# Dealing channel blocks to SBUF partitions so that a transfer's parts walk through neighbouring blocks of HBM

## The chip, the cores and the metric

One core of one Trainium2 chip. The time is the device time of one execution in microseconds; medians are given with the number of runs. Runs carry a state: a run over 1.5% above the fastest of its kernel is called slow, the others fast; a single run on one core has the state "unknown". Each run has its own runs of the kernel before on the same chip beside it; those medians lay between 91.2 and 91.4 us.

## The reference

An im2col with a 3 x 3 window: for each image and channel, nine shifted copies of the 30 x 30 window positions.

```python
batch, c, h, w = (16, 64, 32, 32)          # float32, kernel_size = 3
for i in range(h_out):                      # 30
    for j in range(w_out):                  # 30
        cols[b, :, i * w_out + j] = x[b, :, i:i + 3, j:j + 3].ravel()
# cols: (16, 64 * 9, 900)
```

No arithmetic: 4.19 MB come in, 33.18 MB go out.

## The kernel before

The 1024 channel planes (16 images x 64 channels) are cut into 128 blocks of eight planes. Partition p holds block p. A block is 32,768 B in x and 259,200 B in the output. Two loads bring two planes and then six planes of every block into SBUF. Then, four times, VectorE and ScalarE copy the nine shifted views of two planes per partition into an output tile, and one transfer sends the tile out: one contiguous run of 64,800 B for each partition. Output tiles have two buffers. SyncE issues all six transfers.

```python
x_v = x.rearrange("b (cp c2) h w -> (b cp) (c2 h w)", c2=CPP)                  # CPP = 8
out_v = out.rearrange("b (cp c2 kk) n -> (b cp) c2 (kk n)", c2=CPP, kk=KK)

def load(r0, r1):
    return nc.sync.dma_start(out=in_flat[:, r0 * W : r1 * W],
                             in_=x_v[:, r0 * W : r1 * W])
first = load(0, 2 * H)
load(2 * H, CPP * H)

for c in range(0, CPP, 2):
    out_tile = out_pool.tile([P, 2, KK, HO, WO], x.dtype, name="out_tile")
    # ... cut: ScalarE and VectorE copy the shifted views of planes c and c + 1 ...
    nc.sync.dma_start(
        out=out_v[:, c : c + 2].rearrange("p c n -> p (c n)"),
        in_=out_tile.rearrange("p c kk i j -> p (c kk i j)"),
    )
# ... cut: the first load is moved ahead of the program's start-up barrier ...
```

In the built program every transfer has two plain dimensions on both sides, 128 rows of one run each. For an output (step and count, in elements, slowest first):

```
HBM  [[64800, 128], [1, 16200]]      SBUF  [[16200, 128], [1, 16200]]
```

Of the kernel before, what the change touches and what calls it, by code (L numbers as in the profile page):

```python
# [1 line left out]

# [3 lines left out]


def _im2col(ctx, tc, x, K, out):


    nc = tc.nc
    P = nc.NUM_PARTITIONS

    B, C, H, W = x.shape
    HO = H - K + 1
    WO = W - K + 1
    KK = K * K
    assert out.shape == (B, C * KK, HO * WO)
    CPP = B * C // P
    assert CPP * P == B * C and C % CPP == 0 and CPP % 2 == 0 and K == 3  # L20

    x_v = x.rearrange("b (cp c2) h w -> (b cp) (c2 h w)", c2=CPP)
    out_v = out.rearrange("b (cp c2 kk) n -> (b cp) c2 (kk n)", c2=CPP, kk=KK)

    in_pool = ctx.enter_context(tc.tile_pool(name="in_pool", bufs=1))
    out_pool = ctx.enter_context(tc.tile_pool(name="out_pool", bufs=2))

    ctx.enter_context(tc.manual_schedule())

    in_tile = in_pool.tile([P, CPP, H, W], x.dtype, name="in_tile")  # L30
    in_flat = in_tile.rearrange("p c h w -> p (c h w)")

    def load(r0, r1):

        return nc.sync.dma_start(
            out=in_flat[:, r0 * W : r1 * W],
            in_=x_v[:, r0 * W : r1 * W],
        )

    first = load(0, 2 * H)  # L40
    load(2 * H, CPP * H)

    def planes(c, ki, kj, n, step):

        w = in_tile[:, c, ki : ki + HO, kj : kj + WO]
        part, row, col = [list(d) for d in w.ap]
        return bass.AP(w.tensor, w.offset, [part, [step, n], row, col])

    for c in range(0, CPP, 2):
        out_tile = out_pool.tile([P, 2, KK, HO, WO], x.dtype, name="out_tile")  # L50


        for s in range(2):
            o = out_tile[:, s]
            nc.scalar.copy(out=o[:, K : 2 * K], in_=planes(c + s, 1, 0, K, 1))  # L55
            for ki in (0, 2):
                nc.vector.tensor_copy(  # L57
                    out=o[:, ki * K : ki * K + 2], in_=planes(c + s, ki, 0, 2, 1)
                )
            if s == 0:  # L60
                nc.vector.tensor_copy(  # L61
                    out=o[:, 2:KK:6], in_=planes(c + s, 0, 2, 2, 2 * W)
                )
            else:
                nc.vector.tensor_copy(  # L65
                    out=o[:, 2], in_=in_tile[:, c + s, 0:HO, 2 : 2 + WO]
                )
                nc.scalar.copy(  # L68
                    out=o[:, 8], in_=in_tile[:, c + s, 2 : 2 + HO, 2 : 2 + WO]
                )  # L70
        nc.sync.dma_start(  # L71
            out=out_v[:, c : c + 2].rearrange("p c n -> p (c n)"),
            in_=out_tile.rearrange("p c kk i j -> p (c kk i j)"),
        )
    return first


def kernel(
    tc: tile.TileContext,
    x: bass.AP,  # L80
    kernel_size: bass.AP,
    out: bass.AP,
):
    with ExitStack() as ctx:
        first = _im2col(ctx, tc, x, int(kernel_size), out)


    tc.close()
    tc.compile()  # L89
    blocks = tc.nc.main_func.blocks  # L90
    load = first.ins
    home = next(b for b in blocks if any(i.name == load.name for i in b.instructions))
    home.instructions = [i for i in home.instructions if i.name != load.name]
    head = list(blocks[0].instructions)
    at = next(
        k
        for k, i in enumerate(head)
        if i.engine == load.engine and type(i).__name__ == "InstDrain"
    )
    head.insert(at, load)  # L100
    blocks[0].instructions = head


# [1 line left out]
_INS = ['x', 'kernel_size']  # L105
_OUTS = [((16, 576, 900), 'float32')]

_NUMBERS = {'kernel_size': 3}


# [26 lines left out]
```

## Time and profile before

| | before |
|---|---|
| time, median of 6 runs | 91.19 us (91.10 to 91.30) |
| span of the profiled run | 89.6 us |
| DMA packets of the first load, 8,192 B, mean | 378 ns |
| DMA packets of the second load, 24,576 B, mean | 912 ns |
| DMA packets of the outputs, 64,800 B, mean | 2397 ns |

The packet durations come from the trace's records of single packets: 128 data packets per transfer, eight for each of the 16 engines. They can be checked from any DMA view of a window: (share of 16 engines) x 16 x (length of the window) / (packets). The lines below are the DMA view of the kernel before, from 5 to 11 us, where only the second load runs. The columns of the second line are packets, MB and share.

```profile
DMA packets 108, 2.65 MB, mean 442 GB/s; under 512 B 0, under 2 KB 0, under 8 KB 0
q1 hardware_dynamic: 108, 2.65, 102.6%
```

1.026 x 16 x 6 us / 108 is 0.912 us. (A share can be over 100% because a packet is counted whole where it starts.)

The time from issue to landing, from the page, and the waits of VectorE for a free output buffer (total, times, longest):

```profile
out_dram<-out_tile SPq DMA_DIRECT2D x4, 8100.0 KB, 32.4
in_tile<-in_x_dram SPq DMA_DIRECT2D x1, 3072.0 KB, 11.4
DVE out_tile L57 <- DMA out_dram<-out_tile: 27.1, 2, 13.6
```

An output transfer is under way for 19.15 us; for the rest of the 32.4 us it lay in the queue behind the one before it.

### The profile page before, as it was taken

What the parts mean: (1) busy time and instruction counts of PE and PEld (TensorE: products, weight loads), DVE (VectorE), ACT (ScalarE), POOL (GpSimd) and SP (SyncE); (2) the same over time, 40 slices, a digit from 0 to 9 for tenths busy, and PEclk for the clock granted to TensorE, in tenths of its full rate; (3) what the DMA queues carried; (4) which work ended last, traced back from release to release, by engine and by line L of the source; (5) the groups of instructions that cost most, each with busy time, mean ns of one, the idle gap of its engine ahead of it and who ended that gap; (6) DMA issues with size and microseconds to landing.
All of it is one profiled execution on the core that took longest, in us unless ns stands there. A gap on an engine that the chain in (4) does not pass through costs nothing.

```text
span 89.6 us, 96 instructions
## 1 busy us (share of the span) xinstructions
DVE 22.6 (25%) x24; ACT 23.8 (27%) x13; POOL 0.2 (0%) x4
## 2 busy tenths in 40 slices
DVE  0079759900000099500000399100000000000000
ACT  5079759900000099500000399100000000000000
POOL 0000000000000000000000000000000000000000
DMA  5989899999999999947999999999999982999990
GB/s 128 505 384 494 362 463 463 463 463 463 463 463 463 463 463 463 434 174 318 463 463 463 463 463 463 463 463 463 463 463 463 463 347 116 463 463 463 463 463 0
DMA packets 864, 37.37 MB, mean 417 GB/s; under 512 B 96, under 2 KB 96, under 8 KB 96
## 3 DMA queue, kind: packets, MB, share of 16 engines
q1 hardware_dynamic: 864, 37.37, 97.2%
HBM read 4.19 MB, written 33.18 MB: 417 GB/s over the span
## 4 chain that ended last, share of the span: by engine, by line
DMA 49%; DVE 12%; DVEq 1%; issue 0%; SPq 0%
DMA out_dram<-out_tile 36%; DMA in_tile<-in_x_dram 13%; DVE out_tile L57 8%; DVE out_tile L61 2%; DVE out_tile L65 1%; DVEq L89 1%; DVEq L57 0%; SPq L71 0%
## 5 line engine op out<-in xcount | busy, mean ns | idle before, releaser
L55 ACT COPY out_tile<-in_tile 128x2700 f32<-128x2700 f32 x8 | 19.2, 2443 | 31.7 <-DMA out_dram<-out_tile 27.1
L57 DVE COPY out_tile<-in_tile 128x1800 f32<-128x1800 f32 x16 | 16.8, 1092 | 33.7 <-DMA out_dram<-out_tile 27.1
L61 DVE COPY out_tile<-in_tile 128x1800 f32<-128x1800 f32 x4 | 4.4, 1090 | 0.0
L68 ACT COPY out_tile<-in_tile 128x900 f32<-128x900 f32 x4 | 3.8, 938 | 0.0
L65 DVE COPY out_tile<-in_tile 128x900 f32<-128x900 f32 x4 | 2.5, 620 | 0.0
L55 ACT ACT_TABLE_LOAD x1 | 1.3, 1283 | 0.8 <-PEq L118 0.8
L118 POOL MEMSET const-bfloat16-1.0<- 128x1 bf16 x1 | 0.1, 101 | 0.0
L118 POOL MEMSET const-uint8-127<- 128x1 uint8 x1 | 0.1, 101 | 0.0
L118 POOL MEMSET const-float32-0.0<- 128x1 f32 x1 | 0.1, 98 | 0.2 <-issue 0.2
L118 POOL MEMSET const-float32-1.0<- 128x1 f32 x1 | 0.1, 98 | 0.0
## 6 DMA issues: line engine op xcount, KB each, us to landing
out_dram<-out_tile SPq DMA_DIRECT2D x4, 8100.0 KB, 32.4
in_tile<-in_x_dram SPq DMA_DIRECT2D x1, 3072.0 KB, 11.4
in_tile<-in_x_dram SPq DMA_DIRECT2D x1, 1024.0 KB, 4.9
```

Of the source, the lines that this page charges most:

```text
L55: nc.scalar.copy(out=o[:, K : 2 * K], in_=planes(c + s, 1, 0, K, 1))
L57: nc.vector.tensor_copy(out=o[:, ki * K : ki * K + 2], in_=planes(c + s, ki, 0, 2, 1))
L61: nc.vector.tensor_copy(out=o[:, 2:KK:6], in_=planes(c + s, 0, 2, 2, 2 * W))
L65: nc.vector.tensor_copy(out=o[:, 2], in_=in_tile[:, c + s, 0:HO, 2 : 2 + WO])
L68: nc.scalar.copy(out=o[:, 8], in_=in_tile[:, c + s, 2 : 2 + HO, 2 : 2 + WO])
L89: tc.compile()
L118: nc = _bacc.Bacc("TRN2", target_bir_lowering=False, num_devices=1)
```

## The change

The intent: let the 16 engines work in neighbouring blocks of HBM at each moment instead of eight blocks apart. It assumes that a transfer is cut into sixteen parts of eight neighbouring rows, one part for each engine; the traces show 128 data packets per transfer and the 16 engines busy 97.2% of the span, not which rows an engine takes. Partition 8a+b now owns block 16b+a. The core of the diff:

```diff
-    x_v = x.rearrange("b (cp c2) h w -> (b cp) (c2 h w)", c2=CPP)
-    out_v = out.rearrange("b (cp c2 kk) n -> (b cp) c2 (kk n)", c2=CPP, kk=KK)
+    CP = C // CPP
+    A = 16
+    x_v = x.rearrange("(b1 b0) (cp c2) h w -> (b0 cp) b1 (c2 h w)", b0=A // CP, c2=CPP)
+    out_v = out.rearrange(
+        "(b1 b0) (cp c2 kk) n -> (b0 cp) b1 c2 (kk n)", b0=A // CP, c2=CPP, kk=KK
+    )
...
-            in_=x_v[:, r0 * W : r1 * W],
+            in_=x_v[:, :, r0 * W : r1 * W],
...
-            out=out_v[:, c : c + 2].rearrange("p c n -> p (c n)"),
+            out=out_v[:, :, c : c + 2].rearrange("a b c n -> a b (c n)"),
```

The output transfer is now:

```
HBM  [[64800, 16], [1036800, 8], [1, 16200]]      SBUF  [[16200, 128], [1, 1], [1, 16200]]
```

## The prediction

The prediction and the expectations say "ports" for an assumption: that two parts of a transfer can share something on their way and then take about twice as long. It is the second of the prediction's rivals. No trace or run names a port or tells what is shared. By "the engine's rate" they mean the 27.16 GB/s per engine that the prediction works out from the packet records; what sets this rate, no run shows.

> **What bounds the kernel now.** I read four views in this order: the page (shares of the span), the chain of waits, the waits of the issuing queue beside the timeline of the issues, and the DMA view cut to windows, down to the records of the single packets.

> The page first: the span, the busy shares, the DMA rows, the queue, the bytes.

> ```profile
> span 89.6 us, 96 instructions
> DVE 22.6 (25%) x24; ACT 23.8 (27%) x13; POOL 0.2 (0%) x4
> DMA  5989899999999999947999999999999982999990
> GB/s 128 505 384 494 362 463 463 463 463 463 463 463 463 463 463 463 434 174 318 463 463 463 463 463 463 463 463 463 463 463 463 463 347 116 463 463 463 463 463 0
> q1 hardware_dynamic: 864, 37.37, 97.2%
> HBM read 4.19 MB, written 33.18 MB: 417 GB/s over the span
> ```

> Both compute engines idle three quarters of the time; the 16 DMA engines are busy 97.2% of the span. The dips in the two DMA rows (around slices 18 and 33) are a matter of where a slice's edge falls: a packet is counted where it starts, all engines start a packet almost together, and so a slice may hold none.

> Next the chain that ended last:

> ```profile
> 0.79 11.40 DMA in_tile<-in_x_dram
> 17.95 32.59 DMA out_dram<-out_tile
> 55.77 0.54 DVE out_tile L65
> ```

> The chain names DVE for part of the way, but that is only how it walks back through semaphores. The test is whether the queue ever ran dry, and the waits of the queue with the timeline answer it:

> ```profile
> SPq L71 <- DVE out_tile L65: 54.0, 4, 18.9
> 10.69 46.03 SPq L71 DMA_DIRECT2D out_dram<-out_tile  x4
> ```

> The four output transfers are issued between 10.69 us and 56.7 us. The packet records put the end of the third transfer at 69.1 us, so the fourth lay in the queue for over 12 us before its turn; the second was issued at 17.95 us and started at 30.7. Only the first output is not covered: issued at 10.69, its first packets start at 11.54, while the last packets of the load end between 11.24 and 11.83. There is no room worth having in compute or waits.

> Last, the DMA view of a piece of the output phase:

> ```profile
> DMA packets 64, 4.15 MB, mean 415 GB/s; under 512 B 0, under 2 KB 0, under 8 KB 0
> q1 hardware_dynamic: 64, 4.15, 95.7%
> ```

> That is the window from 20 to 30 us: 64 packets took 95.7% of 16 x 10 us, or 2.39 us each. The single records agree and say more. Each transfer has 128 data packets, one per partition, eight per engine. Output packets of 64,800 B: median 2393 ns, smallest 2388, largest 2433, over all 512. Packets of the second load, 24,576 B: 912 ns, every one of the 128. Packets of the first load, 8,192 B: 309 ns for most, but 20 or so at the start take 324 to 1147 ns.

> Three sizes lie on one straight line: (2393 - 912) ns over (64,800 - 24,576) B is 27.16 GB/s per engine, and with that rate each size leaves about 7 ns fixed (912 - 905; 309 - 302; 2393 - 2386). HBM reads and HBM writes have the same rate and no scatter.[...]

> The sum per engine: mean start 1.18 us; first load 3.02 (8 x 309 = 2.47, plus 0.55 of slow first packets); second load 8 x 0.912 = 7.30; outputs 4 x 8 x 2.397 (the mean) = 76.72; semaphore packets 0.05. That gives 88.27 us, against a last packet at 88.15 to 88.33 us in the records. Another 1.3 us of landing and end make the span of 89.6, and 1.5 us outside it make the 91.12.

> [...]96 semaphore packets over 6 transfers show 16 now.[...]

> **The change part by part.** Removed: nothing; added: nothing. The same two loads and four outputs, copies, waits and buffers. What moves is which channel block lies in which partition: 8p..8p+7 style runs give way to block 16b+a in partition 8a+b. In HBM each packet is the same contiguous run (8,192, 24,576 or 64,800 B). The HBM pattern gets one dimension more, 16 x 8 x run.

> - Output packets: 32 per engine x 2393 ns either way. Best case they lose their scatter, 0.08 us in sum per engine (mean over median). Expected: 0.
> - Second load: 8 x 912 ns, no scatter to lose. Expected: 0.
> - First load: 0.55 us of slow first packets. If these are a start-up latency, they stay. If the 16 engines' first addresses collide in HBM, neighbouring blocks (32 KiB apart in x) may change it either way. I take -0.1, at most -0.55. This is on the path: everything queues behind it.
> - Issue: an issue takes 332 to 382 ns on the queue now, and 1.01 us pass from the first issue to the first packet. [...]only the first issue is on the path (the others have 0 to 12 us of cover): +0.05.
> - Copies: unchanged, 22.6 and 23.8 us, under the DMA.

> Sum: 91.12 - 0.1 + 0.05 = 91.07, say 91.0.

> **The rivals.**

> First, locality in HBM pays: the intent of the change. Against it: [...]packets have no scatter. It can be worth only the start, 0.55 + 0.08: 90.5 us, 0.7% faster, still "same".

> [...]The new HBM pattern has 16 outermost, so the hardware may cut the transfer into sixteen runs of eight partitions, 8a to 8a+7 (as the words of the change suppose)[...].[...] Packets of about 4.8 us, the DMA's 87.1 us twice: about 178 us.[...] Against it: if the present 128 partitions are already cut into such runs, then the present trace shows that it costs nothing[...]. I give this, with milder forms of it, 8%.

> Third, the neighbouring blocks collide in HBM.[...] Were the loads to run at half rate, 10.3 us more: 101 us.[...] I give it 4%.

> Fourth, fewer engines or smaller packets[...]. The run is contiguous as before and two outer dimensions remain; I give it under 1%.

> **Range and chances.** The mechanism leaves 90.5 (all start-up scatter gone) to 91.7 (a slower first load and start by 0.5 us), and the kernel's own runs scatter by 0.1. So 91.0, with a range of 90.5 to 91.7. Faster by over 2% would need 1.8 us, three times what is not already at the engines' rate: 1%. Slower by over 2%: 12%, from the second and third rivals. Within 2%: 87%.

> **What would show it.** Right: the output packets stay at 2.39 us and the second load's at 0.91, the queue's share of the span stays at 97%, four outputs of 19.15 us each follow each other without a gap, and the second output lands about 32 us after its issue. Only the first 3 us may differ. Wrong: packets longer than these. If output packets lie near 4.8 us throughout, it is the ports; if they scatter, or if only the loads are longer, it is HBM; if there are other than 16 semaphore packets per transfer, the split[...].

## The result, and the profile after

| | before | after |
|---|---|---|
| time, median of 6 runs | 91.19 us | 169.31 us (166.97 to 170.51) |
| ratio of the fast runs, 95% interval | | 1.845 (1.834 to 1.857) |
| packets of 8,192 B, mean | 378 ns | 596 ns |
| packets of 24,576 B, mean | 912 ns | 1885 ns |
| packets of 64,800 B, mean (smallest, largest) | 2397 ns (2388, 2433) | 4420 ns (2391, 5346) |

Ratios are the mean time of one kernel's fast runs over that of the other's fast runs of the same rounds, so not quite the ratio of the medians. Three of the six runs of the changed kernel are labelled slow, only because its runs scatter by 2%; the granted clock was 1.0 in all of them.

The page of the changed kernel, as far as it answers to the lines shown of before:

```profile
span 167.3 us, 96 instructions
DVE 22.6 (14%) x24; ACT 23.8 (14%) x13; POOL 0.2 (0%) x4
DMA  7998999999896999998996998898999999699910
GB/s 157 282 188 188 188 496 248 248 248 248 170 186 139 310 186 248 248 248 186 201 232 186 310 217 186 217 310 186 201 217 294 217 248 232 232 279 248 217 62 31
q1 hardware_dynamic: 864, 37.37, 96.4%
HBM read 4.19 MB, written 33.18 MB: 223 GB/s over the span
```

The compute engines did exactly the same work. The DMA engines were again busy nearly all the time (96.4%), with the same 864 packets and the same bytes, at half the rate. So no work was added and the DMA engines did not stand idle: the packets became longer. The busy share counts a packet as busy however long it takes, and so it does not show this.

Now the DMA views of three windows of the changed kernel: 8 to 18 us (second load), 40 to 50 us (first output) and 100 to 150 us.

```profile
DMA packets 93, 2.29 MB, mean 229 GB/s; under 512 B 0, under 2 KB 0, under 8 KB 0
q1 hardware_dynamic: 93, 2.29, 110.4%
...
DMA packets 31, 2.01 MB, mean 201 GB/s; under 512 B 0, under 2 KB 0, under 8 KB 0
q1 hardware_dynamic: 31, 2.01, 98.2%
...
DMA packets 200, 11.92 MB, mean 238 GB/s; under 512 B 16, under 2 KB 16, under 8 KB 16
q1 hardware_dynamic: 200, 11.92, 100.3%
```

The same sum as above gives 1.90 us per packet of the second load, 5.07 us per output packet early on, and later, with 184 data packets (16 of the 200 are semaphore packets), 4.36 us. The records show the same: 1.92 us is the commonest value in the second load, 5.05 us in the outputs. Both are 2.1 times the values of before. One engine then moves 64,800 B / 5.056 us = 12.8 GB/s, and 16 engines 205 GB/s. Later the parts come out of step: the last packet of the first output ended between 54.5 and 55.8 us over the engines, of the last output between 157.3 and 166.2 us.

The issue and the waits, to be held against the lines of before:

```profile
out_dram<-out_tile SPq DMA_DIRECT2D x4, 8100.0 KB, 66.3
in_tile<-in_x_dram SPq DMA_DIRECT2D x1, 3072.0 KB, 21.0
0.00 1.89 SPq L41 DMA_DIRECT2D in_tile<-in_x_dram  x2
DVE out_tile L63 <- DMA out_dram<-out_tile: 60.8, 2, 32.5
```

VectorE's waits more than doubled, but as an effect: it waits for buffers that the transfers release later.

Where the 77.7 us of span come from, per engine in the mean: the first packet starts at 1.54 instead of 1.18 us (+0.36); the first load takes 4.77 instead of 3.02 us (+1.75); the second 15.08 instead of 7.30 (+7.78); the outputs 141.43 instead of 76.72 (+64.71); and the last engine ends 3.36 us after the mean engine instead of 0.10 (+3.26). Together +77.9, with 0.15 us less between the last packet and the end of the span.

### The profile page after: what moved, and what is told of

Its sections match the earlier page's. It is cut to its first block, busy times and chain, and to the rows that moved or that the text cites. A ratio compares the mean times of both kernels' runs of the same rounds, so it can differ in the third digit from the quotient of the medians.

```text
span 167.3 us, 96 instructions
## 1 busy us (share of the span) xinstructions
DVE 22.6 (14%) x24; ACT 23.8 (14%) x13; POOL 0.2 (0%) x4
## 2 busy tenths in 40 slices
DMA packets 864, 37.37 MB, mean 223 GB/s; under 512 B 96, under 2 KB 96, under 8 KB 96
## 3 DMA queue, kind: packets, MB, share of 16 engines
q1 hardware_dynamic: 864, 37.37, 96.4%
HBM read 4.19 MB, written 33.18 MB: 223 GB/s over the span
## 4 chain that ended last, share of the span: by engine, by line
DMA 30%; another core or an unknown queue 19%; DVE 10%; DVEq 1%; issue 0%; SPq 0%
DMA out_dram<-out_tile 26%; DVE out_tile L63 7%; DMA in_tile<-in_x_dram 4%; DVE out_tile L67 2%; DVE out_tile L71 1%; DVEq L95 1%; DVEq L63 0%; SPq L77 0%
## 5 line engine op out<-in xcount | busy, mean ns | idle before, releaser
L71 DVE COPY out_tile<-in_tile 128x900 f32<-128x900 f32 x4 | 2.5, 623 | 0.0
```

What stands on the lines that cost most here:

```text
L71: nc.vector.tensor_copy(out=o[:, 2], in_=in_tile[:, c + s, 0:HO, 2 : 2 + WO])
```

## The experiments

Three theories were open.

- **Ports.** A transfer whose HBM side has 16 outermost is cut into sixteen runs of eight neighbouring partitions, and parts that work 32 partitions apart then slow each other.
- **HBM.** Sixteen parts in neighbouring blocks collide there.
- **Form.** The third dimension, or the longer way of issuing that goes with it, is slow by itself. An issue took 332 to 382 ns on the queue before, and 538 to 667 ns after.

"Round" below means the n-th packet of a transfer on each engine.

### 1. The longer issue alone

```diff
     nc = tc.nc
+    nc.dge_precook = False
```

> The kernel before, with one change: the compiler's short form of issue is switched off. The changed kernel lost this form too (its two loads' issues took 1.89 us together, 1.12 before), so the way of issuing is a rival of its own. Ports theory[...]: packets stay at 2393 ns, the time rises only by the slower first issue, about 91.6 us. HBM theory (neighbouring blocks in step collide): the same, 91.6. Issue-form theory: packets near 5 us, about 167.

Measured: 92.88 us (one run), correct. Output packets 2391 to 2433 ns. The issue did become longer, as in the changed kernel:

```profile
0.00 1.70 SPq L36 DMA_DIRECT2D in_tile<-in_x_dram  x2
```

The form of issue does not slow the output packets. It costs 1.6 us, more than I had put down (0.4): the first packet starts at 1.34 instead of 1.01 us, some packets of the second load take up to 1745 ns, and the last engine begins its output at 13.36 instead of 11.84 us. Why packets of the second load (28 of its 128 took over 950 ns) become longer here is open.

### 2. Neighbouring places in HBM, the old pattern

Loads in the same manner, so the result is wrong.

```diff
-            out=out_v[:, c : c + 2].rearrange("p c n -> p (c n)"),
+            out=bass.AP(out.tensor, out.offset + (c // 2) * P * N2, [[N2, P], [1, N2]]),
```

> The result is wrong on purpose. The transfers keep the two-dimensional pattern of before (128 runs), but partition p goes to the p-th of 128 runs that lie one behind the other, so that the parts work in neighbouring places of HBM (about 259 KB apart or two times that, as in the changed kernel). Ports theory: packets stay at 2393 and 912 ns, 91.2 us, within 0.5% of before. HBM theory: packets of 4.8 to 5.3 us, 150 to 170 us. If locality is worth anything with clean ports, this run shows it: at most 0.6 us.

Measured: 91.34 us, median of 5, ratio 1.0013 (0.9999 to 1.0027). From 20 to 30 us:

```profile
DMA packets 64, 4.15 MB, mean 415 GB/s; under 512 B 0, under 2 KB 0, under 8 KB 0
q1 hardware_dynamic: 64, 4.15, 95.7%
```

2.39 us per packet. All packets of the second load took 912 ns. So with this pattern closeness in HBM neither hurts nor helps, and the intended gain of the change did not appear.

### 3. The new pattern, far apart in HBM

Again a wrong result; the loads likewise.

```diff
-            out=out_v[:, c : c + 2].rearrange("p c n -> p (c n)"),
+            out=bass.AP(out.tensor, out.offset + (16 * (c // 4) + c // 2 % 2) * N2,
+                        [[32 * N2, 16], [2 * N2, 8], [1, N2]]),
```

> The result is wrong on purpose. The HBM pattern is 16 x 8 runs, as in the changed kernel, but a part's first runs lie eight blocks from the next part's (2,073,600 B in the output, 262,144 B in x), far apart, as sixteen equal pieces of the old order do. Ports theory: as slow as the changed kernel, packets mostly 5.06 us (1.92 us in the second load), 160 to 172 us. HBM theory: 91 to 93 us.

Measured: 169.54 us (one run), as the changed kernel. From 40 to 50 us:

```profile
DMA packets 32, 2.07 MB, mean 207 GB/s; under 512 B 0, under 2 KB 0, under 8 KB 0
q1 hardware_dynamic: 32, 2.07, 101.0%
```

5.05 us per packet. Runs 2 and 3 together take the addresses out of the question: the shape 16 x 8 x run carries the whole loss.

### 4. Half of the partitions at a time, old addresses

```diff
-        nc.sync.dma_start(out=out_v[:, c : c + 2]..., in_=out_tile...)
+        for h in (0, P // 2):
+            nc.sync.dma_start(out=out_v[h : h + P // 2, c : c + 2]...,
+                              in_=out_tile[h : h + P // 2]...)
```

> Correct result. Patterns and addresses of the kernel before, but each output goes out as two transfers, partitions 0 to 63 and then 64 to 127[...]. Loads stay as before (packets of 912 ns). Ports theory: output packets of about 5.06 us, as most of the changed kernel's, 10.3 + 32 x 5.06 = 172 and 4 us of start and end, so 155 to 178 us[...]. HBM theory: 91 to 94 us, for addresses are the old ones.

Measured: 167.36 us (one run), correct. The loads kept 912 ns; from 40 to 50 us the outputs show

```profile
DMA packets 32, 2.07 MB, mean 207 GB/s; under 512 B 0, under 2 KB 0, under 8 KB 0
q1 hardware_dynamic: 32, 2.07, 100.5%
```

The median packet took 5.056 us. Halving the partitions of a transfer gives the same packet length as the new pattern does in step (5.05 us), with no third dimension and at the old addresses. What slows the packets is not shown by this run.

### 5 to 8. Which outer size spoils it

Runs 5 to 7 use the same kind of permutation with another outer size A (partition (128/A)a+b owns block A·b+a; all correct). Run 8 has 128 outermost and two shorter runs per partition, `[[4 * N2, P], [N2, 2], [1, N2 // 2]]`, with the SBUF side cut in two as well and the loads as before (wrong).

```diff
-            out=out_v[:, c : c + 2].rearrange("p c n -> p (c n)"),
+            out=bass.AP(out.tensor, out.offset + c * KK * HO * WO,
+                        [[BO, A], [A * BO, 128 // A], [1, 2 * KK * HO * WO]]),   # A = 8, 32, 64
```

For runs 6 and 7 two outcomes stood against each other: packets as slow as in the changed kernel, 165 to 171 us, or packets at 2393 ns with the longer issue, 92.5 to 93.5 us.

> Correct result. Partition 16a+b owns block 8b+a: the HBM pattern is 8 x 16 runs.[...] If parts are runs of neighbouring partitions and share ports in pairs[...]: 37.37 MB at 4 x 25.6 GB/s (25.6 is twice 24,576 B in 1.92 us, from the changed kernel) are 365 us, packets of about 5.06 us, 330 to 370 us in all. If ports play no role, eight engines at 27.1 GB/s: packets of 2393 ns, 172 us and 4 more, about 176 us. If sixteen engines work after all: about 167.

> Correct result. Partition 4a+b owns block 32b+a: the HBM pattern is 32 x 4 runs. If a part is always a sixteenth in order (eight neighbouring partitions), as slow as the changed kernel, 165 to 171 us. [...]packets stay at 2393 ns and the time is that of the plain issue, 92.5 to 93.5 us.

> Correct result. Partition 2a+b owns block 64b+a: the HBM pattern is 64 x 2 runs. If parts are sixteenths in order whenever the outer size of HBM's side isn't 128: 165 to 171 us. [...]92.5 to 93.5 us.

> The result is wrong on purpose. The output's HBM pattern has three dimensions too, but with 128 outermost: each partition writes two runs of 32,400 B that lie 64,800 B apart. If it is the outer size that spoils the dealing, packets stay at the engine's rate, 32,400 B in about 1200 ns, and the time is 91 to 93 us. If any third dimension does it: packets of about 2.5 us, 165 to 171 us.

| HBM side | time (one run; the change: median of 6) | median output packet |
|---|---|---|
| 8 x 16 x run | 302.07 us | 4648 ns |
| 16 x 8 x run (the change) | 169.31 us | 4865 ns |
| 32 x 4 x run | 93.12 us | 2391 ns |
| 64 x 2 x run | 92.62 us | 2395 ns |
| 128 x 2 x half run | 91.66 us | 1204 ns for 32,400 B |

The view of run 6 from 20 to 30 us shows the full rate:

```profile
DMA packets 64, 4.15 MB, mean 415 GB/s; under 512 B 0, under 2 KB 0, under 8 KB 0
q1 hardware_dynamic: 64, 4.15, 95.7%
```

With 32 or 64 outermost, the blocks are permuted in the same manner as in the change, there is a third dimension, the long issue is used (1.88 us for the two loads in both, 1.12 before), and yet the output packets run at full rate, 2391 and 2395 ns. The 1.2 to 1.7 us above the kernel before are about what the long issue cost in run 1 (1.6). Run 8 has the third dimension too, with 128 outermost (and kept the short issue, 372 to 403 ns). So it is neither the third dimension nor the permutation. The slow patterns are those in which one outer row holds eight or more neighbouring partitions; as there are 128 partitions in all, these runs can't tell that from a small outer size. Runs 9 and 10 do.

Run 5 was slower than the change but faster than I expected (330 to 370). The page shows why the first and explains the second in part:

```profile
q1 hardware_dynamic: 816, 37.37, 48.8%
```

816 packets are 768 data packets and 48 semaphore packets, eight for each of the six transfers, where the changed kernel has 96, and the share is 48.8% of 16 engines: eight engines worked. Packets in step lay at 4.9 to 5.2 us, but 117 of the 512 output packets ran at under 2.45 us (40 in the changed kernel). I take it that eight parts came out of step more than I had allowed for; no run shows it by itself.

### 9 and 10. The distance of 32 partitions

Eight engines in both; 8 x 4 runs over 32 partitions against 8 x 8 runs over 64 partitions. Loads as before, order of the outputs wrong.

```diff
+        for g in range(0, P, G):                               # G = 32 or 64
+            nc.sync.dma_start(
+                out=bass.AP(out.tensor, out.offset + g * BO + c * KK * HO * WO,
+                            [[BO, 8], [8 * BO, G // 8], [1, 2 * KK * HO * WO]]),
+                in_=out_tile[g : g + G].rearrange("p c kk i j -> p (c kk i j)"))
```

> The result is wrong on purpose (loads as before, outputs in a permuted order). Each output goes out as four transfers of 32 partitions with an HBM pattern of 8 x 4 runs: eight engines, [...]no two partitions that are 32 apart are under way together. Ports theory: no sharing, packets of 2391 ns, 64 in a row on each of eight engines: 12 + 153 + 3, about 168 us. If the slow packets come from the sixteen-way or eight-way pattern as such: packets near 5 us, about 300 us.

> The result is wrong on purpose. As the run with 8 x 4 runs, but two transfers of 64 partitions with 8 x 8 runs: eight engines again[...]. Ports theory: most packets 4.9 to 5.1 us, 64 in a row, with some drift as in the run with 8 x 16: 280 to 335 us. If 32 partitions of distance do not matter: as the other run, about 168 us.

Measured: 168.77 us and 301.70 us (one run each). From 100 to 150 us, first the run with 32 partitions, then the one with 64:

```profile
DMA packets 208, 10.89 MB, mean 218 GB/s; under 512 B 40, under 2 KB 40, under 8 KB 40
q1 hardware_dynamic: 208, 10.89, 50.4%
```

```profile
DMA packets 98, 5.83 MB, mean 117 GB/s; under 512 B 8, under 2 KB 8, under 8 KB 8
q1 hardware_dynamic: 98, 5.83, 49.7%
```

Without the semaphore packets, 168 and 90 data packets in the same time: 2.40 us and 4.42 us. Both fill half the time of 16 engines, 50.4% and 49.7%. The number of engines is the same, the pattern has the same outer size, the destination is equally far apart; what differs is that a transfer of the second holds partitions 32 apart and one of the first does not. So an outer size of 8 is not slow in itself. The two runs differ in one more thing, an outer row of four partitions against one of eight; but run 4 has no such rows and shows the same 5.06 us. The distance alone is not enough either: a transfer of the kernel before holds partitions 32 apart too, and its packets take 2.39 us. Which partitions the engines work on at one time may decide it; that is not shown, for no trace tells which partitions an engine takes.

### 11. The change's order with packets at full rate, timed

The kernel of run 6 again.

> Correct result; the 32 x 4 pattern again, timed. It keeps the change's order of neighbouring blocks[...]. Since the run with neighbouring runs in a two-dimensional pattern gained nothing, I expect only the slower issue: 92.6 to 93.2 us, ratio 1.015 to 1.022.

Measured: 92.92 us, median of 5, ratio 1.0178 (1.0164 to 1.0193), as expected. Even in a form with packets at full rate, an order of this kind loses 1.6 us, about what the longer issue cost in run 1, and gains nothing. None of the kernels beats the one before, and nothing here pointed to one that would.

### 12. The new pattern for the outputs alone

Loads as before. Its output is wrong, which doesn't matter for the time.

```diff
-            out=out_v[:, c : c + 2].rearrange("p c n -> p (c n)"),
+            out=bass.AP(out.tensor, out.offset + c * KK * HO * WO,
+                        [[BO, 16], [16 * BO, 8], [1, 2 * KK * HO * WO]]),
```

> The result is wrong on purpose. Outputs with the changed kernel's pattern of 16 x 8 runs, loads as before. The change's two loads cost 1.75 and 7.78 us more per engine, so without them the time should be 169.1 - 9.5, about 159.5 us, with output packets of 4.42 us in the mean. Besides: in all three runs with contended loads the first two rounds of the first output ran at full rate (2.4 to 2.6 us), in the two runs with clean loads they did not. If contended loads bring those rounds about, here the first round lies near 5 us, and the time is up to 5 us longer, 160 to 165; if the 16 x 8 pattern itself does, they are fast here too.

Measured: 167.81 us (one run). Both numbers were too low: repairing the loads, 9.5 us per engine, bought 1.3 us against the profiled run of the change, and the change's own runs scatter by more than that (166.97 to 170.51 us). The traces show where the gain went: to an odd piece of the changed kernel. Its first output ran two rounds nearly undisturbed, as the view from 23.6 to 26 us shows (16 packets, 2.39 us each):

```profile
DMA packets 16, 1.04 MB, mean 432 GB/s; under 512 B 0, under 2 KB 0, under 8 KB 0
q1 hardware_dynamic: 16, 1.04, 99.7%
```

In run 12 the first round lies at 4.73 to 5.06 us, as in runs 4 and 10, where the loads were clean too. From 11.5 to 31.5 us run 12 shows 64 data packets (6 of the 70 are semaphore packets) of 5.05 us each:

```profile
DMA packets 70, 4.15 MB, mean 207 GB/s; under 512 B 6, under 2 KB 6, under 8 KB 6
q1 hardware_dynamic: 70, 4.15, 101.0%
```

The first output took 39.9 us there, 34.1 us in the changed kernel, and the engines' ends spread wider (the last 6.5 us after the mean, 3.4 in the changed kernel). So a part of the loads' loss was already given back in the first output. The two fast rounds follow slow loads in all three such kernels (the change, runs 3 and 5) and clean loads in none (runs 4, 10 and 12), and run 12 differs from the change in its loads alone; each is one profile. Why is open, and it bears on the cause: in the second round all 16 packets took 2391 to 2396 ns, so nothing slowed them there. In the first four rounds of that output an engine moved 4 x 64,800 B in about 14.8 us, 17.5 GB/s, against 12.8 GB/s for packets in step, so one fixed rate per engine does not describe the pattern.

## Why the prediction was wrong

The prediction said 91.0 us (90.5 to 91.7) and gave 12% to "slower". Measured: 169.31 us.

The signs listed at the end of the prediction worked in part: "If output packets lie near 4.8 us throughout, it is the ports; if they scatter ... it is HBM". In the event they did both, and it was not HBM: run 3, with far addresses, scatters just as much (2391 to 5301 ns). It took the experiments to tell the two apart.

## What to carry to other kernels

The DMA engines were busy 97% of the time here with output packets of one length, and a new order in HBM gained nothing (run 2: ratio 1.0013); what mattered was how long the packets took under the new access pattern. For a transfer of 128 partitions, 128 outermost on both sides was the fastest form here (91.2 to 91.7 us with the short issue); keep it unless a run shows better. Here 64 or 32 kept the packet rate too, at the price of the longer issue (92.6 to 93.1 us); with 16, all engines were still busy 96% of the time and the transfers ran at about half the rate. Read packet durations, not busy shares: the output packets went from 2397 to 4420 ns in the mean while the busy share went from 97.2 to 96.4%.
